# A one-core hybrid layer in split fp32: GpSimd's block sums spread over two stages, the branch product's first operands issued by GpSimd, its gates loaded three groups ahead

## The chip, the cores and the metric

The kernel runs on one core of a Trainium2 chip. The metric is the device time of one execution in microseconds (us). Five engines run side by side, each in its own order: TensorE (PE), VectorE (DVE), ScalarE (ACT), GpSimd (POOL) and SyncE (SP), which here does nothing but issue DMA transfers. GpSimd issues transfers too, among them all that add to what is in memory (accumulating DMA). The transfers themselves run on 16 DMA engines that all issuers share.

## The reference

One layer of a streaming encoder, for a prompt of 1024 frames and a sample of 32, with model width 1024, all in float32:

```
h = RMSNorm(x)
z = h @ W_in -> [q_A k_A v_A | q_B f_B i_B og_B | gate_A gate_B]
A: windowed grouped-query attention on q_A k_A v_A            -> y_A
B: HGRN2 gated linear recurrence, 8 heads of width 128        -> y_B
m = sigmoid(gate_A) * (y_A @ W_brA) + sigmoid(gate_B) * (y_B @ W_brB)
x = x + RMSNorm(m @ W_out)
[a|u] = RMSNorm(x) @ W_up;  a = causal conv3(a)
x = x + RMSNorm((gelu(a) * u) @ W_down)                       (d_ff = 2816)
x = x + (p @ W_ple) * sigmoid(x @ W_ple_gate)
```

Besides x it returns the last window rows of k and v, the recurrence's final states and the convolution's tail.

## The kernel before

Each fp32 product is made of three matmuls on split operands (high by high, high by low, low by high). The large products also use a block scheme of seven products for a 2 by 2 block matrix in place of eight, so that some operands are sums of blocks of a weight or of an activation. Most weight sums are made on VectorE and GpSimd from tiles that were loaded. For W_down, for the branch weight W_brA and for y_A, they are made by GpSimd's DMA instead: a transfer with an adding write puts them into tensors in memory, `w_d` (W_down, 704 KB a transfer), `wa_d` (W_brA, 1024 KB) and `sa_d` (y_A, whose tensor is `ya_d`, 1056 KB). `dv`, `av` and `ya_v` are views of W_down, W_brA and y_A by blocks.

The stages in time, by the profile:
- to about 350 us: norm, attention and the first gates (tiles `ya`, `hs`, `gt`; the stores `tb_d<-gt`, `ta_d<-gt`). Per pair of heads `ya` is stored to `ya_d`, and its negated halves to `sa_d`;
- 353 to 857 us: stage B. Eight heads, each a unit of products for q and f, one for i and og, and the recurrence in blocks. The program is a list `pieces` of product steps; `at(m, f)` hangs a small job on piece m. Each unit's weights come by `b_raw` (L1027, tile `wu`, 512 KB each, on SP), are summed and split, and VectorE makes from the products the tiles `tf`, `vt`, `qx` and the state `S`. GpSimd zeroes tiles (`tq`, `d`, `kk`), copies part of `ke`, loads `S` and issues the sums;
- 857 to 869 us: the last three gate units, `stream(tail[3:], small)`, where `small` hangs jobs on half units: loads (`a_load`) and splits (`a_split`) of the first operands `oa` of the branch product, and weights (`a_prepare`);
- from 876 us: the branch product (`a_unit`; matmuls at L1597 to L1601 into `st`), whose gates come back from memory by `a_gate` as `ta`;
- 1060 to 1200: W_out and the mix; 1200 to 1616: the up stage, 22 units of about 20 us (`up_unit`); then down, and from 1850 the per-layer input.

The order on each engine is set by the order in which the program is written and by a scheduler; `behind(E, V, G)` keeps an instruction behind the last ones written for those engines, as an order and without a semaphore. GpSimd so runs ahead until an instruction of its own has to wait. Of the 45 sums in stage B, 32 are of W_down (four parts `c` of eight sums `n`), at piece 8 + 5(4n + c); 13 are of y_A and W_brA, at piece 10 + 12n. The lines that set this:

```
for n, (o, a, h, other) in enumerate(w_sums):
    for c in range(4):
        ...
        at(8 + 5 * (4 * n + c), w_sum)
...
    at(10 + 12 * n, a_sum)
```

Of the kernel before, what the change touches and what calls it, by code (L numbers as in the profile page):

```python
# [10 lines left out]
F32 = mybir.dt.float32  # L11
# [6 lines left out]
P = 128  # L18
# [12 lines left out]
H = 264  # L31
# [28 lines left out]
def layer_kernel(  # L60
# [229 lines left out]
    def gtile():  # L290
        return lp.tile([P, GMAX], F32, tag="gt", name=nm("gt"), bufs=2)
# [25 lines left out]
    with right("ap") as ap:  # L317
# [226 lines left out]
        def values(i, js):  # L544

            kv, ya = i // 4, yas[i]
            o = o8.pop(i) if js[0] == 8 else o_bank()
            m_ = span(js[0])[0]
            for x, j in enumerate(js):
                ph, pl = probs.pop((i, j))  # L550
                tl = span(j)[4]
                oc = o[:, x * 256:x * 256 + 2 * m_]
                for a, (vt_, _, _) in enumerate(tl):
                    lhs = Vs[:, vt_, kv].rearrange("p a b -> p (a b)")
                    z = slice(2 * a * m_, 2 * (a + 1) * m_)
                    E.matmul(oc, lhs, ph[:, z], start=a == 0, stop=False)
                    E.matmul(oc, lhs, pl[:, z], start=False, stop=a == len(tl) - 1)
            nx = len(js)
            u = aq.tile([P, 2, 2, P], F32, tag="u", name=nm("u"), bufs=1)
            o4 = o[:, :nx * 2 * m_].rearrange("p (x h q) -> p x h q", x=nx, h=2)  # L560
            t0 = 1024 if js[0] == 8 else js[0] * P
            y3 = ya[:, t0:t0 + nx * m_].rearrange("p (x q) -> p x q", x=nx)
            S.copy(u[:, :nx, :, :m_], o4)
            V.tensor_tensor(y3[0:64], o4[0:64, :, 0, :], u[64:128, :nx, 0, :m_], op=ALU.add)
            V.tensor_tensor(y3[64:128], o4[64:128, :, 1, :], u[0:64, :nx, 1, :m_], op=ALU.add)
            if js[-1] == 8:
                dma(ya_d[:, i], ya[:])
                for p in range(2):
                    nt, o = gtile(), H * (2 * p + 1 - i // 4)
                    S.mul(nt[:, :H], ya[:, o:o + H], -1.0)  # L570
                    for q in ((4, 3) if i < 4 else (5,)):
                        dma(sa_d[q][:, i % 4, p], nt[:, :H])

        def h_sums(k):


            hs = [aq.tile([P, 384], F32, tag=f"hs{a}", name=nm("hs")) for a in range(4)]
# [508 lines left out]
    with right("bp") as bp:  # L1086
# [351 lines left out]
        def more():  # L1438
# [4 lines left out]
        at(len(pieces) - 2, more)  # L1443
        w_sums = [(3, 0, 0, None), (4, 0, 1, None), (1, 0, 0, None), (6, 1, 0, None),
                  (3, 0, 1, None), (4, 1, 1, None), (1, None, None, 4), (6, None, None, 1)]
        for n, (o, a, h, other) in enumerate(w_sums):
            for c in range(4):
                def w_sum(o=o, src=w_d[other][:, c] if other else dv[:, a, h, c], c=c,
                          op={"accum_op": ALU.add} if n > 3 else {}):
                    with behind(E, V, G):  # L1450
                        gdma(w_d[o][:, c], src, **op)
                at(8 + 5 * (4 * n + c), w_sum)
        a_sums = [(3, av[:, 0, 0], 0), (4, av[:, 0, 1], 0), (1, av[:, 0, 0], 0), (6, av[:, 1, 0], 0),
                  (3, av[:, 0, 1], 1), (4, av[:, 1, 1], 1), (1, wa_d[4][:], 1), (6, wa_d[1][:], 1)]
        y_sums = [(4, ya_v[:, 0, 0], 1), (3, ya_v[:, 1, 1], 1), (1, sa_d[4][:], 0),
                  (1, ya_v[:, 1, 1], 1), (5, sa_d[1][:], 1)]
        for n, (dst, (o, src, acc)) in enumerate([(sa_d, y) for y in y_sums] + [(wa_d, a) for a in a_sums]):
            def a_sum(dst=dst[o], src=src, op={"accum_op": ALU.add} if acc else {}):
                with behind(E, V, G):
                    gdma(dst[:], src, max_dma_last_dim=4224, **op)  # L1460
# [62 lines left out]

    opa = {}

    def a_load(i, p):
        t = opa[i, p] = page_at(at_a[i][p], [P, 2, 4, H], "oa")
        src = sa_d[i][:, :, p] if i in sa_d else ya_v[:, min(i, 1), i // 6][:, :, p]
        dma(t[:, 1].bitcast(F32), src)

    def halves(hi, lo):
        S.copy(hi, lo.bitcast(F32))
# [18 lines left out]
    pctx.close()  # L1551
# [3 lines left out]
    with right("mp") as mp:  # L1555
# [11 lines left out]
        Ra, Rb, Ya, Yb = [None] * 4, [None] * 4, [None] * 4, [None] * 4  # L1567
        R_ = page_at("l6", [P, 4, 2, H], "R").bitcast(F32)

        def a_gate(col, h, sl):  # L1570
            t = mp.tile([P, 2, H], F32, tag="ta", name=nm("ta"), bufs=4)
            dma(t[:, sl], ta_d[col].rearrange("p (t h c) -> p h t c", t=2, h=2)[:, h, sl])
            return t

        def a_unit(ph, c, tps=(0, 1), ws=None, beside=None):
# [9 lines left out]
            for n, i in enumerate(OPS[ph]):  # L1585
                if ws is None:
                    a_prepare(n_a[0] + 5)
                    w = ready_a[n_a[0]]
                    n_a[0] += 1
                else:  # L1590
                    w = ws[n]
                kept.append(w)
                t, first = banks[i]
                for p in tps:
                    o, x = t[:, p, 0:H], opa[i, p]
                    for k in range(4):
                        E.matmul(o, w[:, 0, k], x[:, 0, k], start=first and k == 0, stop=False,  # L1597
                                 skip_group_check=True)
                        E.matmul(o, w[:, 0, k], x[:, 1, k], start=False, stop=False,
                                 skip_group_check=True)  # L1600
                        E.matmul(o, w[:, 1, k], x[:, 0, k], start=False, stop=k == 3,  # L1601
                                 skip_group_check=True)
                x, r = t[:, sl, 0:H], R_[:, c, sl]
                if i == 0:
                    d["s"], d["ta"] = tmp("as"), a_gate(c, 0, sl)
                    S.copy(d["s"][:, sl], x)
                elif i == 1:
                    V.tensor_tensor(r, x, d["s"][:, sl], op=ALU.subtract)
                elif i == 2:
                    ta = d["ta"]  # L1610
                    V.scalar_tensor_tensor(ta[:, sl], ta[:, sl], 1.0, x, op0=ALU.add, op1=ALU.mult)
                    gdma(mx_d[:, 0, c, sl], ta[:, sl])
                elif i == 3:
                    d["c"] = tmp("ac")
                    V.tensor_tensor(d["c"][:], r, x, op=ALU.subtract)
                elif i == 4:
                    e, ta = d["c"], a_gate(c + 4, 1, sl)
                    V.tensor_tensor(e[:], e[:], x, op=ALU.subtract)
                    V.scalar_tensor_tensor(ta[:], ta[:], 1.0, e[:], op0=ALU.add, op1=ALU.mult)
                    gdma(mx_d[:, 1, c], ta[:])  # L1620
                else:
                    e, ta = tmp("ac"), a_gate(*((c + 4, 0) if i == 5 else (c, 1)), sl)
                    V.tensor_tensor(e[:], *((r, x) if i == 5 else (x, r)), op=ALU.subtract)
                    V.scalar_tensor_tensor(M_[i][:, c], ta[:], 1.0, e[:], op0=ALU.add, op1=ALU.mult)
                if beside:
                    beside(n)
            return kept

        steps_a = {}

        def during(s, f, *a):
# [19 lines left out]
        for n, (i, p) in enumerate(((1, 1), (2, 1), (3, 0), (3, 1))):  # L1651
            during(n + n // 2, both, a_split, i, p)
# [606 lines left out]
    def up_unit(u):  # L2259
# [62 lines left out]
        for ps, steps in (((0,), first_), ((1,), early)) if u == 0 else (((0, 1), order),):  # L2322
            for n, (i, t, first, then) in enumerate(steps):
# [518 lines left out]
```

## Time and profile before

| | |
|---|---|
| median of 3 runs (lowest, highest) | 1982.41 us (1981.38, 1985.9) |
| the profiled execution | 1977.89 us, span 1976.2 us |
| its mean granted TensorE clock | 0.994 |
| busy: PE, DVE, ACT, POOL | 1935.5, 1452.8, 1011.4, 300.8 us |
| moved by DMA | 302.19 MB, mean 153 GB/s |

The profile is of one execution. Its rows name an engine, a line (L1027), an operation and the tiles out<-in. In a timeline, a bracket at the end of a row is the idle time of that engine ahead of the instruction and what ended it. A row of waits gives the waiting engine and line, what it waited for, and the total, count and longest in us. In the chain that ended last a row gives a start, a length and the work. A row by stretches gives the limits, the length, the busy time of the engines, then the granted clock (1.00 is full), the mean busy share of the DMA engines and GB/s. "SPq" is a queue that issues DMA; a row with x2 stands for two issues and their joint time.

### The profile page before, as it was taken

The numbers are of one execution on the slowest core, as the hardware profiler recorded it, in microseconds if no ns is written. First come the engines' busy times: TensorE is split into PE (matmuls) and PEld (weight loads), VectorE is DVE, ScalarE is ACT, GpSimd is POOL, SyncE is SP. The second block draws the span as 40 slices with busy tenths as digits, with TensorE's granted clock in tenths as the row PEclk, the third lists the DMA queues.
The fourth block names the chain that finished last, engine by engine and source line by source line (L and its number), as shares of the span: only waits on it lengthen the run. The fifth ranks groups of instructions, "written<-read, shape, count | busy, mean of one in ns | idle before, by whom it ended". The sixth has DMA issues, their size and how long they took to land.

```text
span 1976.2 us, 38048 instructions
## 1 busy us (share of the span) xinstructions
PE 1935.5 (98%) x14619; PEld 1916.4 (97%) x14619; DVE 1452.8 (74%) x3160; ACT 1011.4 (51%) x2182; POOL 300.8 (15%) x414
## 2 busy tenths in 40 slices
PE   8999999899999999989999999999999999999998
PEld 8999999899999999989999999999999999999998
DVE  6777777688888788747755678877878786668872
ACT  7667777466666656644223664333333345534432
POOL 2111211011112100000001023233343320000000
PEclk9999999999999999989999999999999999999999
DMA  8544544745749942268757583332333347655443
GB/s 267 150 114 115 138 128 104 213 114 170 160 109 159 176 108 73 90 219 271 212 158 264 166 306 103 108 110 87 119 99 110 109 142 253 206 186 160 118 133 88
DMA packets 311403, 302.19 MB, mean 153 GB/s; under 512 B 14293, under 2 KB 278904, under 8 KB 311221
## 3 DMA queue, kind: packets, MB, share of 16 engines
q1 hardware_dynamic: 279909, 232.27, 37.9%
q0 software_dynamic: 31184, 67.43, 14.5%
q8 instruction: 115, 1.88, 0.4%
q14 instruction: 67, 0.55, 0.1%
q10 hardware_dynamic: 128, 0.06, 0.0%
HBM read 213.48 MB, written 115.16 MB: 166 GB/s over the span
## 4 chain that ended last, share of the span: by engine, by line
PE 77%; DVE 9%; DMA 6%; ACT 4%; issue 3%; POOL 0%; SPq 0%; ACTq 0%; DVEq 0%; POOLq 0%
PE st L2278 7%; PE st L2276 7%; PE st L2277 7%; PE mm L205 5%; PE mm L207 5%; PE mm L206 5%; PE st L2395 4%; PE st L2397 4%; PE st L2396 4%; DMA wu<-in_w_in_dram 2%; PE G L1121 2%; PE G L1120 2%; PE G L1118 2%; PE Y L1118 2%; PE Y L1121 2%
## 5 line engine op out<-in xcount | busy, mean ns | idle before, releaser
L2276 PE MATMUL st<-op,wt 128*128 128x264 f32 x1232 | 349.0, 283 | 2.5 <-ACT Sp L2287 1.4
L2278 PE MATMUL st<-op,wt 128*128 128x264 f32 x1232 | 349.9, 284 | 0.0
L2277 PE MATMUL st<-op,wt 128*128 128x264 f32 x1232 | 347.9, 282 | 0.0
L2276 PEld LDWEIGHTS st<-op,wt 128*128 128x128 f32 x1232 | 231.3, 188 | 4.0 <-ACT Sp L2287 2.0
L2277 PEld LDWEIGHTS st<-op,wt 128*128 128x128 f32 x1232 | 231.4, 188 | 0.0
L2278 PEld LDWEIGHTS st<-op,wt 128*128 128x128 f32 x1232 | 230.9, 187 | 0.0
L2395 PE MATMUL st<-dop,wt 128*128 128x264 f32 x616 | 174.5, 284 | 1.2 <-ACT S L2410 1.2
L2397 PE MATMUL st<-dop,wt 128*128 128x264 f32 x616 | 174.4, 283 | 0.0
L2396 PE MATMUL st<-dop,wt 128*128 128x264 f32 x616 | 174.0, 283 | 0.0
L1944 ACT CAST wt<-wu 128x512 fp32r<-128x512 f32 x126 | 75.9, 618 | 178.1 <-POOL ab L2262 75.5
L205 PE MATMUL mm<-La,wh 128*128 128x384 f32 (+1 forms) x480 | 158.5, 331 | 0.4 <-DVE pl L229 0.4
L206 PE MATMUL mm<-Lb,wh 128*128 128x384 f32 (+1 forms) x480 | 155.3, 324 | 0.6 <-DVE Lb L780 0.6
L207 PE MATMUL mm<-La,wl 128*128 128x384 f32 (+1 forms) x480 | 155.0, 323 | 0.1
L1945 DVE TENSOR_TENSOR wt<-wu,wt 128x512 fp32r<-128x512 f32 x126 | 86.4, 694 | 46.7 <-ACT wt L1944 46.7
L2395 PEld LDWEIGHTS st<-dop,wt 128*128 128x128 f32 x616 | 115.6, 188 | 1.6 <-ACT S L2410 1.4
L2396 PEld LDWEIGHTS st<-dop,wt 128*128 128x128 f32 x616 | 115.7, 188 | 0.0
L2397 PEld LDWEIGHTS st<-dop,wt 128*128 128x128 f32 x616 | 115.5, 188 | 0.0
L2050 ACT CAST wt<-wd 128x512 fp32r<-128x512 f32 (+1 forms) x84 | 49.1, 586 | 91.2 <-PE st L2397 69.5
L1039 ACT CAST wt<-wu 128x512 fp32r<-128x512 f32 x108 | 64.8, 617 | 58.1 <-DVE wu L1047 25.3
L1040 DVE TENSOR_TENSOR wt<-wu,wt 128x512 fp32r<-128x512 f32 x108 | 72.5, 685 | 27.2 <-ACT wt L1039 26.9
L206 PEld LDWEIGHTS mm<-Lb,wh 128*128 128x128 f32 x480 | 90.5, 189 | 1.7 <-DVE Lb L780 1.4
L205 PEld LDWEIGHTS mm<-La,wh 128*128 128x128 f32 x480 | 90.3, 188 | 0.7 <-DVE pl L229 0.6
(600 smaller groups left out, 6294.0 us busy)
## 6 DMA issues: line engine op xcount, KB each, us to landing
wu<-in_w_up_dram SPq DMA_DIRECT2D x42, 512.0 KB
wu<-in_w_in_dram SPq DMA_DIRECT2D x36, 512.0 KB
w_d<-in_w_down_dram POOLq DMA_DIRECT2D x24, 704.0 KB, 11.0
a_d<-Up SPq DMA_DIRECT2D x22, 528.0 KB
wr<-in_w_in_dram SPq DMA_DIRECT2D x21, 512.0 KB
s_d<-sm SPq DMA_DIRECT2D x40, 264.0 KB
dop<-s_d SPq DMA_DIRECT2D x16, 528.0 KB
wr<-in_w_out_dram SPq DMA_DIRECT2D x16, 512.0 KB
```

The costliest lines, as they stand in the source:

```text
L205: E.matmul(ps, wh, a, start=first and n == 0, stop=False)
L206: E.matmul(ps, wh, b, start=False, stop=False)
L207: E.matmul(ps, wl, a, start=False, stop=last and n == len(ks) - 1)
L1118: E.matmul(o, wh, x[0][k], start=first and k == 0, stop=False, skip_group_check=True)
L1121: E.matmul(o, wl, x[0][k], start=False, stop=k == 3, skip_group_check=True)
L1945: V.tensor_tensor(t[:, 1], src, t[:, 0].bitcast(F32), op=ALU.subtract)
L2276: E.matmul(o, wh, xh, start=first and k == 0, stop=False, skip_group_check=True)
L2277: E.matmul(o, wh, xl, start=False, stop=False, skip_group_check=True)
L2278: E.matmul(o, wl, xh, start=False, stop=k == 3, skip_group_check=True)
L2395: E.matmul(o, wh, xh_, start=first and k == 0, stop=False, skip_group_check=True)
L2396: E.matmul(o, wh, xl_, start=False, stop=False, skip_group_check=True)
L2397: E.matmul(o, wl, xh_, start=False, stop=k == ng - 1, skip_group_check=True)
```

## The change

Four things are changed.

1. The sums in stage B. 16 of the 32 W_down sums (parts 0 and 1) stay in stage B, interleaved with the other 13 in one list, a sum every 5.5 pieces from piece 26 to 180. The other 16 (parts 2 and 3) go to the up stage, one in each of the units 2 to 17. All have `max_dma_last_dim=4224` now, so that a `w_d<-w_d` sum is cut into rows of 704 elements and not of 1408.
2. The first five operands of the branch product are issued by GpSimd, ahead of the last gate units. The other three stay on SP and are issued beside those units. The splits (`a_split`) come one half unit earlier, five of them instead of four in this stretch.
3. `a_gate` holds a queue: the gates of three groups are loaded ahead, and it is filled again after each group.
4. The negated halves of `ya` use the buffers of `hs` instead of those of `gt`.

```diff
-                    nt, o = gtile(), H * (2 * p + 1 - i // 4)
+                    nt = aq.tile([P, GMAX], F32, tag=f"hs{p}", name=nm("nt"), bufs=1)
+                    o = H * (2 * p + 1 - i // 4)
...
-        for n, (o, a, h, other) in enumerate(w_sums):
-            for c in range(4):
-                def w_sum(o=o, src=..., c=c, op={"accum_op": ALU.add} if n > 3 else {}):
-                    with behind(E, V, G):
-                        gdma(w_d[o][:, c], src, **op)
-                at(8 + 5 * (4 * n + c), w_sum)
+        def block_sum(dst, src, acc):
+            with behind(E, V, G):
+                gdma(dst, src, max_dma_last_dim=4224, **({"accum_op": ALU.add} if acc else {}))
+        def w_sum(n, c):
+            o, a, h, other = w_sums[n]
+            block_sum(w_d[o][:, c], w_d[other][:, c] if other else dv[:, a, h, c], n > 3)
...
+        sums = [lambda n=n, c=c: w_sum(n, c) for n in range(8) for c in range(2)]
         for n, (dst, (o, src, acc)) in enumerate(... y_sums ... a_sums ...):
-            def a_sum(...): ...
-            at(10 + 12 * n, a_sum)
+            sums.insert(2 * n, lambda d=dst[o][:], src=src, acc=acc: block_sum(d, src, acc))
+        for n, f in enumerate(sums):
+            at(26 + 11 * n // 2, f)
...
-    small = {0: [lambda i=i, p=p: a_load(i, p) for p in range(2) for i in range(3)]}
-    small[0] += [lambda p=p: a_load(3, p) for p in range(2)]
-    for m in range(4):
-        p, i = divmod(m, 3)
-        small.setdefault(m + 2, []).append(lambda i=i, p=p: both(a_split, i, p))
-    for m in range(3):
-        small.setdefault(m + 1, []).insert(0, lambda m=m: both(a_prepare, m))
+    first_a = [(i, p) for p in range(2) for i in range(3)]
+    for i, p in first_a[:5]:
+        a_load(i, p, gdma)
+    for m, (i, p) in enumerate(first_a[:5]):
+        small[m + 1] = [lambda i=i, p=p: both(a_split, i, p)]
+    for m in range(3):
+        small[m + 1].append(lambda m=m: both(a_prepare, m))
+    for m, (i, p) in enumerate(((2, 1), (3, 0), (3, 1))):
+        small[m + 3].append(lambda i=i, p=p: a_load(i, p))
...
-        def a_gate(col, h, sl):
+        def a_gate(col, h, tps):
+            while len(ta_a) < 3 and gates_a:
+                c_, h_, p_ = gates_a.pop(0)
+                t = mp.tile([P, 2, H], F32, tag="ta", name=nm("ta"), bufs=4)
+                ...
+                ta_a.append(((c_, h_, p_), t))
...
+                if 2 <= u < 18 and n == 4:
+                    w_sum((u - 2) // 2, 2 + u % 2)
```

What it does to the order is shown at three places. A row is a line, an operation and the tiles with their running numbers, in the order in which the engine takes them.

GpSimd at the first head of stage B (`tq`, `d` are zeroed tiles, `ke` is the copy that PE transposes later). Before:

```order
L1451 DMA w_d_131<-in_w_down_dram 128x11x128
L1460 DMA sa_d_110<-ya_d 1024x1x264
L1451 DMA w_d_131<-in_w_down_dram 128x11x128
L1254 MEMSET tq_5070 128x96
L1451 DMA w_d_131<-in_w_down_dram 128x11x128
L1460 DMA sa_d_109<-ya_d 1024x1x264
L1451 DMA w_d_131<-in_w_down_dram 128x11x128
L1451 DMA w_d_132<-in_w_down_dram 128x11x128
L1254 MEMSET d_949_5369 128x96
L1303 COPY ke_5370<-vt_5286 128x32
```

After:

```order
L1255 MEMSET tq_5070 128x96
L1449 DMA sa_d_110<-ya_d 1024x1x264
L1255 MEMSET d_949_5366 128x96
L1304 COPY ke_5367<-vt_5283 128x32
L1255 MEMSET tq_5560 128x96
L1449 DMA w_d_131<-in_w_down_dram 128x11x128
```

Seven sums stood ahead of the copy, one does now.

GpSimd at head 4, from one copy of `ke` to the next. Before:

```order
L1303 COPY ke_8273<-vt_8189 128x32
L1254 MEMSET tq_8463 128x96
L1311 MEMSET kk_8575 32x128
L1312 MEMSET kk_8575 64x128
L1460 DMA wa_d_106<-in_w_br_a_dram 512x1x512
L1451 DMA w_d_130<-w_d_132 128x1408
L1460 DMA wa_d_104<-wa_d_106 256x1024
L1451 DMA w_d_130<-w_d_132 128x1408
L1451 DMA w_d_133<-w_d_130 128x1408
L1324 DMA S_8795<-in_state_hgrn_dram 128x128
L1451 DMA w_d_130<-w_d_132 128x1408
L1254 MEMSET d_1550_8941 128x96
```

After:

```order
L1304 COPY ke_8259<-vt_8174 128x32
L1255 MEMSET tq_8447 128x96
L1449 DMA w_d_132<-in_w_down_dram 128x11x128
L1312 MEMSET kk_8559 32x128
L1313 MEMSET kk_8559 64x128
L1449 DMA w_d_131<-in_w_down_dram 128x11x128
L1325 DMA S_8778<-in_state_hgrn_dram 128x128
L1449 DMA wa_d_106<-in_w_br_a_dram 512x1x512
L1255 MEMSET d_1550_8924 128x96
L1449 DMA wa_d_104<-wa_d_106 256x1024
L1304 COPY ke_8925<-vt_8805 128x32
L1449 DMA w_d_130<-w_d_132 128x2x704
```

Six sums became four, and the load of the state S comes ahead of two of them.

ACT at the start of the branch product (`oa` casts are the splits of its operands, `wt` those of its weights, `gt` the last three gates, the third of which frees the bank that the first branch matmul writes). Before:

```order
L297 ACTIVATE gt_10904<-X_10863 128x288
L1532 CAST oa_10876<-oa_10876 128x1056
L297 ACTIVATE gt_10946<-Y_10916 128x384
L1532 CAST oa_10878<-oa_10878 128x1056
L1532 CAST oa_10880<-oa_10880 128x1056
L297 ACTIVATE gt_10984<-Z_10957 128x384
L1532 CAST oa_10882<-oa_10882 128x1056
```

After (weights' casts in between, as before, not shown):

```order
L297 ACTIVATE gt_10882<-X_10857 128x288
L1534 CAST oa_10847<-oa_10847 128x1056
L297 ACTIVATE gt_10926<-Y_10896 128x384
L1534 CAST oa_10849<-oa_10849 128x1056
L1534 CAST oa_10851<-oa_10851 128x1056
L1534 CAST oa_10853<-oa_10853 128x1056
L297 ACTIVATE gt_10968<-Z_10939 128x384
L1534 CAST oa_10855<-oa_10855 128x1056
```

The last gate now stands behind four casts of operands, all four loaded by GpSimd, where it stood behind three. On SP the store `tb_d<-gt` of the first of these gates now stands behind one load of `oa` instead of eight.

More of the change, by code (lines that the diff above doesn't have):

```diff
@@ L574, in h_sums @@
         def h_sums(k):
-            hs = [aq.tile([P, 384], F32, tag=f"hs{a}", name=nm("hs")) for a in range(4)]
+            hs = [aq.tile([P, GMAX], F32, tag=f"hs{a}", name=nm("hs"), bufs=1) for a in range(4)]
             b11, b12, b21, b22 = (t[:] for t in hs)
@@ L1568, in layer_kernel @@
         R_ = page_at("l6", [P, 4, 2, H], "R").bitcast(F32)
-        def a_gate(col, h, sl):
-            t = mp.tile([P, 2, H], F32, tag="ta", name=nm("ta"), bufs=4)
-            dma(t[:, sl], ta_d[col].rearrange("p (t h c) -> p h t c", t=2, h=2)[:, h, sl])
+        tps_a = [(0, (0,)), (1, (0,)), (0, (1,)), (1, (1,)), (2, (0, 1)), (3, (0, 1))]
+        gates_a = [(c, 0, tps) for c, tps in tps_a]
+        gates_a += [(a, h, (0, 1)) for c in range(4) for a, h in ((c + 4, 1), (c + 4, 0), (c, 1))]
+        ta_a = []
+        def a_gate(col, h, tps):
+            while len(ta_a) < 3 and gates_a:
+                c_, h_, p_ = gates_a.pop(0)
+                t = mp.tile([P, 2, H], F32, tag="ta", name=nm("ta"), bufs=4)
+                z_ = slice(p_[0], p_[-1] + 1)
+                dma(t[:, z_], ta_d[c_].rearrange("p (t h c) -> p h t c", t=2, h=2)[:, h_, z_])
+                ta_a.append(((c_, h_, p_), t))
+            if col is None:
+                return
+            key, t = ta_a.pop(0)
+            assert key == (col, h, tuple(tps))
             return t
@@ L1604, in a_unit @@
                 if i == 0:
[L1605 removed]
+                    d["s"] = tmp("as")
                     S.copy(d["s"][:, sl], x)
@@ L1627, in a_unit @@
             return kept
+        a_gate(None, 0, ())
         steps_a = {}
@@ L1650, in layer_kernel @@
             during(9 + n + n // 2, both, a_split, i, p)
-        for n, (i, p) in enumerate(((1, 1), (2, 1), (3, 0), (3, 1))):
-            during(n + n // 2, both, a_split, i, p)
+        for n, (i, p) in enumerate(((2, 1), (3, 0), (3, 1))):
+            during(2 * n + 1, both, a_split, i, p)
         for n in range(4):
```

17 lines of the change are left out of this document (7 added, 10 removed).

## The prediction

> **What bounds the kernel now.** I read the page first (span, engines, granted clock), then the waits of TensorE (PE), then the chain that ended last, and then the timeline around each wait that is both long and near something the change touches.
>
> ```profile
> span 1976.2 us, 38048 instructions
> PE 1935.5 (98%) x14619; PEld 1916.4 (97%) x14619; DVE 1452.8 (74%) x3160; ACT 1011.4 (51%) x2182; POOL 300.8 (15%) x414
> ```
>
> PE is busy for 1935.5 of 1976.2 us. The change removes no matmul, so all it can win is idle time, 40.7 us in the whole kernel, and the half-speed stretches that idle time brings. The waits of PE, with the line and operation that each was waiting for:
>
> ```profile
> PE st L1597 <- ACT gt L297: 7.8, 1, 7.8
> PE so L1367 <- DVE S L1347: 5.5, 2, 4.8
> PE Z L1118 <- DVE tf L1146: 5.1, 1, 5.1
> ...
> PE Y L1118 <- DVE vt L1139: 2.2, 1, 2.2
> ```
>
> They are single places (a 5.5 that is one of 4.8 and a small one). The chain that ended last puts a late DMA at the three longest:
>
> ```profile
> 359.86 20.29 DMA wu<-in_w_in_dram
> ...
> 682.28 10.97 DMA out_dram<-S
> ...
> 867.43 8.49 DMA tb_d<-gt
> ```
>
> So this is a kernel at its matmuls' pace with three holes, at 376, 689 and 869 us, all made by late transfers. I price each hole and then what the moved work could cost where it goes.
>
> **The change, hole one: the first head of stage B (first GpSimd sums).** The rows below are SP's, POOL's (GpSimd's), ACT's and PE's own, then two stretches with PE busy time, granted clock, DMA share and GB/s, and the size of a wu load.
>
> ```profile
> 359.33 19.05 SPq L1027 DMA_DIRECT2D wu<-in_w_in_dram  x4
> 355.96 1.45 POOL L1460 DMA_DIRECT2D sa_d<-ya_d  x1 [17.83 <-DMA ya_d<-ya]
> 356.97 2.59 POOL L1451 DMA_DIRECT2D w_d<-in_w_down_dram  x2
> 378.63 0.62 ACT L1039 CAST wt<-wu 128x512 fp32r<-128x512 f32 x1 [10.49 <-DMA wu<-in_w_in_dram]
> 381.48 0.66 PE L1118 MATMUL Z<-La,wt 128*128 128x384 f32 x1 [5.12 <-DVE tf L1146]
> 397.68 0.44 PE L1118 MATMUL Y<-TH,wt 128*128 128x384 f32 x1 [2.15 <-DVE vt L1139]
> 383.09:386.51 3.42, 3.42 (x13) 0.50 0.01 2
> 386.51:389.92 3.41, 3.41 (x24) 1.00 0.00 0
> wu<-in_w_in_dram SPq DMA_DIRECT2D x36, 512.0 KB
> ```
>
> GpSimd issues one ya sum and two w_down sums at 356 to 359.6 us, just as SP issues four loads of wu; the cast needs wu and has it at 378.6, 19 us later. In the new order GpSimd issues a single sum ahead of the copy of ke of this head, and that one already stands before the 355.96 wait; the one in the row above and both w_down sums come only after the copy. The wait therefore loses its cause: four loads of 512 KB (2.1 MB), at the 358 GB/s that a crowded stretch reaches further below, take 5.9 us from 359.3, and were wanted by about 373.5 (381.48 less 5.12 less the 2.85 from cast to matmul). Saved: 5.1 us of wait. The clock fell to 0.50 after that idle time and the matmuls from 381.48 to 386.51 ran at half speed: 5.0 us that would take 2.5, so 2.5 more. The vt wait at 397.7 is VectorE still catching up with the late wu; I give back 1.0 of its 2.15 (bounds 0 and 2.15). Term one: 5.1 + 2.5 + 1.0 = 8.6.
>
> The Trainium skill, "TensorE: Matmul & The Clock Gate", Part 1, says that the clock is halved after an idle window of 3.4 us, returns after a busy one, and that these windows run freely. The rows above agree: the grid of 3.41 us fits the changes of the clock, and the share at half speed ends on it. It gives the same 2.5 us.
>
> **Hole two: head 4.**
>
> ```profile
> 666.81 4.58 SPq L1027 DMA_DIRECT2D wu<-in_w_in_dram  x2
> 671.12 2.00 POOL L1451 DMA_DIRECT2D w_d<-w_d  x2
> 682.28 0.36 SPq L1352 DMA_DIRECT2D out_dram<-S  x1
> 693.36 0.35 DVE L1347 SCALAR_TENSOR_TENSOR S<-S,dec,so 128x128 f32<-128x128 f32 x1 [6.72 <-DMA out_dram<-S]
> 693.76 0.80 PE L1367 MATMUL so<-z,z 128*128 128x128 f32 x2 [4.85 <-DVE S L1347]
> 672.00:692.00 20.00, 16.91 (x113) 16.56 (x111) 13.34 (x43) 14.91 (x38) 2.76 (x5) 1.00 1.06 228
> 693.71:697.12 3.41, 3.36 (x13) 0.50 0.34 92
> 659.78 0.49 PE L1367 MATMUL so<-vk,am 128*128 128x128 f32 x2 [0.61 <-DVE S L1347]
> ```
>
> The state's small store out_dram<-S is issued at 682.28 and lands 11 us later, because it stands behind two wu loads and five sums that crowd the engines (DMA share 1.06 over 20 us at only 228 GB/s). VectorE may not overwrite S before that, and PE waits 4.85. In the new order four sums stand between the copies of ke of this head and the next instead of six, with the load of S ahead of two of them, and the w_d<-w_d sums come behind the second copy, in rows of 704 elements (2,816 B) instead of 1408. Over stage B the sums fall from 45 in 163 pieces to 29 in 155. I take the wait as gone: 4.85, plus 0.6 at 659.78 (same cause), plus 3.4 us at half clock, worth 1.7. Term two: 7.1; bounds 0 (it merely moves to the next cluster) and 7.2.
>
> **Hole three: the start of the branch product.**
>
> ```profile
> 864.00:876.00 12.00, 4.80 (x28) 4.48 (x26) 4.89 (x5) 4.24 (x6) 0.00 (x0) 0.80 1.10 358
> 867.16 1.08 ACT L1532 CAST oa<-oa 128x1056 fp32r<-128x1056 f32 x1
> 876.02 0.49 ACT L297 ACTIVATE gt<-Z 128x384 f32<-128x384 f32 x1 [7.79 <-DMA tb_d<-gt]
> 868.47 0.34 PE L207 MATMUL Z<-La,wl 128*128 128x384 f32 x1
> 876.57 0.59 PE L1597 MATMUL st<-oa,wt 128*128 128x264 f32 x1 [7.76 <-ACT gt L297]
> 878.02:881.44 3.42, 3.42 (x18) 0.50 0.85 229
> 890.91 0.43 DVE L1611 SCALAR_TENSOR_TENSOR ta<-ta,st 128x264 f32<-128x264 f32 x1 [4.07 <-DMA ta<-ta_d]
> 894.20 0.36 PE L1597 MATMUL st<-oa,wt 128*128 128x264 f32 x1 [0.65 <-DVE R L1608]
> oa<-ya_d SPq DMA_DIRECT2D x6, 528.0 KB
> ```
>
> The first branch matmul waits for the last gate (gt from Z), whose buffer is held by tb_d<-gt, a store that SP issues behind eight loads of 528 KB (0.54 MB). The engines are full at 358 GB/s, so the loads themselves take 8 x 1.51 = 12.1 us. The change gives five to GpSimd and puts the store on SP behind one load only. But ACT's new order has the casts of four GpSimd loads ahead of that gate, one more than before. If the two queues share the engines evenly, the fourth GpSimd load lands after 4 x 3.02 = 12.1 us from 860.6, at 872.7; cast 1.08 and gate 0.5 make PE start at about 874.3 instead of 876.6. Saved: 2.2, and 0.5 of the slow clock (4.87 us at half speed become some 3.7). Gates three groups ahead remove the 4.07 that VectorE waited for ta and the 0.65 that PE waited after it: 0.65. Term three: 3.4. Bounds: 0.6 (loads land no sooner) and 10.2 (GpSimd's four get the full rate and land at 866.7, so PE only waits for Z and its gate, 869.4: 7.2 + 2.4 + 0.6). I take the even split, since no row here shows one queue preferred.
>
> Against this part speaks the Trainium skill, "DMA: Bandwidth & Descriptors", Rules for kernel authors: it says that spreading transfers over several issuing engines does not help bandwidth, since all use the same 16 DMA engines, and saves only issue time. The 358 GB/s at a DMA share of 1.10 agrees with it here. By it alone the sum would lose 2.7 of term three; what it leaves out is which transfer comes first.
>
> **What the moved work costs elsewhere.** Sixteen w_down sums go to the up stage, one each in 16 units.
>
> ```profile
> 407.00 1.05 POOL L1451 DMA_DIRECT2D w_d<-in_w_down_dram  x1
> 1301.98 1.29 POOL L1958 TENSOR_TENSOR wu<-wu 128x512 f32<-128x512 f32 x1 [3.94 <-DVE wt L1945]
> 1300.00:1350.00 50.00, 50.00 (x416) 50.00 (x415) 40.74 (x65) 16.32 (x25) 16.03 (x11) 1.00 0.32 110
> w_d<-in_w_down_dram POOLq DMA_DIRECT2D x24, 704.0 KB, 11.0
> 406.57 0.37 POOL L1303 COPY ke<-vt 128x32 f32<-128x32 f32 x1 [46.83 <-DVE d L1257]
> ```
>
> An issue holds GpSimd for 1.05 us, and behind it in the unit stand only a memset and L1958, which idles 3.94 us first; 0.72 MB in 20 us is 36 GB/s more on a stage at 110, whose DMA share is 0.32. Cost 0, cover 2.9 us; if the cover is gone the up matmuls wait by what exceeds it. Bounds: -1 and +21 (below). Copies of ke that now stand behind sums: the copy above waited 46.83 us for its data and GpSimd had nothing else to do, so cost 0; a late one would show as a wait of PE at L1305. The negated ya halves leave the ring of gt tiles for two of the hs buffers: 0, bounds -1 and +1, since the list of waits shows none of PE in attention above a microsecond. Down: same bytes, 0.
>
> The sum is 8.6 + 7.1 + 3.4 = 19.1 us. The profiled execution took 1977.9 us (span 1976.2 and 1.7 around it), which is 0.23% under the median of the runs, 1982.4. It would become 1958.8. Taken from the median: 1963.3 us.
>
> **Rivals.** (A) GpSimd's loads get the engines almost alone and hole three closes but for the gate: 10.2 instead of 3.4, sum 25.9, 1956.5 us. For it: SP's competing loads also wait for room in its own queue, as the 4.58 us for two wu issues shows. Against: three oa loads of SP's are still there.
> (B) The fourth GpSimd load lands only with the last of the eight, its cast and the gate come when they do now, and term three is 0.65: sum 16.4, 1966.0 us. For it: the 358 GB/s, which no order of issue raises; against: the store that the gate waits for no longer queues behind eight loads. It is what the rule on spreading would give.
> (C) Head 4 still collides: the new order has wa_d sums and w_d<-w_d sums next to each other there, and the second waits for the first to land. If they crowd the wu loads as at 672 to 692, 5 us of term two stay: sum 14.1, 1968.3 us. Against: two of the six sums are gone from that stretch, and the long rows with them.
> (D) The change does not do what it says: the wu loads are late because of their own 2.1 MB and head 4 because of S's load, and the sum is about 0 to 3: 1980 to 1982. Against: 2.1 MB in 19 us is 0.11 TB/s, far below 358 GB/s.
> (E) The other side: in the up stage the issue hits GpSimd where the next unit's weights wait for it. Each of the 16 units would have to lose over 1.2 us to eat 19.1; this begins only when issue and descriptor work exceed 3.94 us a unit. At 5.3 us (3.94 plus 1.35) it would cost 16 x 1.35 = 21.6, so 1984.9 us. Against: 1.05 us in the row, and no wait of PE for GpSimd in the list.
>
> **How the numbers follow.** Main case 0.44, A 0.20, B 0.13, C 0.14, D 0.05, E 0.04. The likeliest gives 1963. Two in ten may lie outside: D and E with 0.09, and the outer parts of A and C; the bounds of single terms, and 0.2% for the level of the runs (1981.4 to 1985.9, which is also about what a measurement of this kernel can tell from no change), widen 1956.5 to 1953 and 1968.3 to 1972. Faster by over 0.2% is main, A, B, C and the near part of D, 0.92; within 0.2% the rest of D, 0.04; slower is E, 0.04.
>
> **What would show it.** After the change PE should have no wait at its matmul of Z for tf near 376 and the loads of wu there should be under 10 us; out_dram<-S near 682 should land within 4 us and no half-clock stretch follow; the first branch matmul should wait for gt some 5 us (main), under 1 (A) or 7 to 8 (B); no wait for ta; the up stage should keep its 20 us a unit with PE at 50.00 of 50 us. The prediction is wrong if a new wait of PE for ke, for wu in the up stage or for the ya halves in attention appears with more than 2 us, or if the hole of head 4 is back at another head.

## The result, and the profile after

The changed kernel takes 1954.43 us (median of 4 runs, 1954.02 to 1955.39) against 1982.12 (median of 4, 1981.38 to 1985.9): a ratio of 0.9857, 95% interval 0.984 to 0.9874, 27.7 us less. It is inside the range and below the forecast of 1963 by 8.6. Its profiled execution took 1954.29 us (span 1952.5).

The page of the changed kernel (span and busy time) and the list of its PE waits:

```profile
span 1952.5 us, 38068 instructions
PE 1929.3 (99%) x14619; PEld 1911.8 (98%) x14619; DVE 1452.2 (74%) x3160; ACT 1012.4 (52%) x2182; POOL 308.5 (16%) x419
```

```profile
PE st L1616 <- ACT gt L297: 5.0, 1, 5.0
PE tr L744 <- POOL ident masks.py:199: 2.6, 1, 2.6
PE st L2297 <- ACT Sp L2308: 1.4, 2, 1.0
PE st L2418 <- ACT S L2433: 1.2, 1, 1.2
PE tr L2816 <- ACT xs L2811: 1.1, 1, 1.1
PE Y L1119 <- DVE vt L1140: 1.0, 1, 1.0
```

Of the long waits of before, tf (5.1) and S (4.8) are gone from the list, vt fell from 2.2 to 1.0, and the gate at the branch's start from 7.8 to 5.0. PE is also 6.2 us less busy (1935.5 to 1929.3) with the same number of matmuls. Most of that is time at half clock: by the clock's records 13.3 us of PE's busy time ran at half speed before and 3.1 us now, and half of the difference is 5.1 us.

Both programs issue the same 14,619 matmuls, in one order but for a dozen that stand a few places off. So the start of the same matmul can be taken from two traces, and the difference tells where the time went. The table gives the length of stretches between such matmuls, for all kernels of this study (the columns' limits in the time of before; up: 1200 to 1626; the branch column runs on to 1173, so that what is won at its start and lost later cancels). It is worked out from the traces' start times, so that each place is compared with itself:

```
us                 0-72  72-218  339-375  375-407  652-714   859-901  859-1173      up
                  start  attent.  B start hole one hole two  branch   branch+
before            69.85  145.53    36.30    32.01    62.73    41.63    313.94   425.58
before, again     68.21  145.53    36.31    35.39    63.12    42.17    314.48   425.57
changed           68.89  144.60    35.16    23.20    55.14    37.68    309.99   425.60
sums_only         68.21  145.53    35.15    22.76    55.13    40.48    312.79   425.60
loads_only        68.95  145.94    36.63    33.88    64.09    39.37    311.68   425.55
neg_gates_only    70.18  144.62    35.51    33.45    63.38    40.85    313.16   425.55
rows_only         69.36  145.51    36.16    32.12    62.98    42.00    314.31   425.57
spread_old_rows   68.22  144.59    35.15    22.78    55.13    37.83    310.19   425.58
late_start        69.70  145.36    35.56    22.78    64.77    40.99    313.30   425.58
up_double         68.50  144.58    35.16    22.78    55.14    38.72    311.02   425.53
gate_first        69.81  144.60    35.16    22.78    55.13    37.71    310.02   425.56
weights_first     67.80  144.61    35.15    22.78    55.13    40.66    317.77   426.24
five_on_sp        69.43  144.58    35.16    22.78    55.13    35.70    309.52   425.55
weights_ahead     69.54  144.73    35.16    22.79    55.13    37.50    310.37   425.54
```

From before to changed: start 1.0 (it differs by 2.4 among the kernels without any change there, so this is scatter), attention 0.9, start of stage B 1.1, hole one 8.8, hole two 7.6, branch 4.0, the rest within 0.1: together 23.4 of the 23.7 by which the span fell. The branch's 4.0 has the most scatter after the start: to 901 us the kernels in which neither its loads nor its gates were changed differ by 1.7 (40.48 to 42.17).

The places in the changed kernel. Hole one: a stretch (PE, PEld, DVE, ACT, POOL busy, clock, DMA share, GB/s) before and after, GpSimd's timeline after, and ACT's casts of wu after.

```profile
362.00:378.00 16.00, 14.35 (x92) 14.12 (x90) 7.85 (x12) 5.05 (x9) 0.00 (x0) 1.00 1.09 254
```

```profile
362.00:378.00 16.00, 16.00 (x104) 16.00 (x103) 12.72 (x21) 9.56 (x16) 0.00 (x0) 1.00 0.28 80
```

```profile
394.75 0.37 POOL L1304 COPY ke<-vt 128x32 f32<-128x32 f32 x1 [60.60 <-DVE d L1258]
...
395.60 1.14 POOL L1449 DMA_DIRECT2D w_d<-in_w_down_dram  x1 [0.32 <-issue]
```

```profile
364.50 1.14 ACT L1040 CAST wt<-wu 128x512 fp32r<-128x512 f32 x2
```

The stretch that moved 254 GB/s at a DMA share of 1.09 now moves 80 at 0.28, PE is busy for all of it, the next sum comes only behind the copy of ke, at 395.6, and ACT has the second pair of wu at 364.5 without a wait, 8.5 us after SP began to issue (355.98).

Hole two: SP's store of S, the next write of S by VectorE, and the stretch around the store's issue.

```profile
669.60 0.36 SPq L1353 DMA_DIRECT2D out_dram<-S  x1
```

```profile
673.87 0.33 DVE L1348 SCALAR_TENSOR_TENSOR S<-S,dec,so 128x128 f32<-128x128 f32 x1
```

```profile
648.00:672.00 24.00, 24.00 (x165) 23.93 (x163) 18.19 (x51) 17.71 (x46) 4.07 (x5) 1.00 0.44 81
```

The store lands within the 4.3 us up to the write (the row has no bracket: nothing was waited for); it took 11 us before. The 20 us that began at 672 before begin, from the same matmul on, at 659 now: PE is busy for all of them, and the engines move 97 GB/s at a share of 0.50, after 228 at 1.06.

Hole three: ACT, PE, two stretches of 3.41 us (PE busy, clock, DMA share, GB/s), and the landing times of GpSimd's five loads.

```profile
852.85 1.07 ACT L1534 CAST oa<-oa 128x1056 fp32r<-128x1056 f32 x1 [0.63 <-DMA oa<-ya_d]
853.83 0.48 ACT L297 ACTIVATE gt<-Z 128x384 f32<-128x384 f32 x1
```

```profile
854.37 0.59 PE L1616 MATMUL st<-oa,wt 128*128 128x264 f32 x1 [4.97 <-ACT gt L297]
```

```profile
851.00:854.41 3.41, 0.04 (x1) 0.94 1.05 357
854.41:857.82 3.41, 3.41 (x17) 0.56 0.96 275
```

```profile
DMA to landing us min/median/max: 4.7/7.5/10.6
```

As priced, the last gate stands directly behind the cast of the fourth GpSimd load, which waits for its DMA, and PE behind the gate. At half speed PE is now busy for 3.1 us (in the clock's window from 854.0 to 857.4) instead of 4.9.

### The profile page after: what moved, and what is told of

The parts are those of the page before. It is cut to its first block, busy times and chain, and to the rows that moved or that the text cites. A ratio compares the mean times of both kernels' runs of the same rounds, so it can differ in the third digit from the quotient of the medians.

```text
span 1952.5 us, 38068 instructions
## 1 busy us (share of the span) xinstructions
PE 1929.3 (99%) x14619; PEld 1911.8 (98%) x14619; DVE 1452.2 (74%) x3160; ACT 1012.4 (52%) x2182; POOL 308.5 (16%) x419
## 4 chain that ended last, share of the span: by engine, by line
PE 86%; DVE 5%; DMA 3%; ACT 3%; issue 2%; POOL 0%; SPq 0%; ACTq 0%; DVEq 0%; POOLq 0%
PE st L2299 7%; PE st L2298 7%; PE st L2297 7%; PE mm L205 6%; PE mm L206 6%; PE mm L207 6%; PE st L2418 4%; PE st L2420 4%; PE st L2419 4%; PE Y L1119 2%; PE G L1122 2%; PE st L205 2%; PE G L1121 2%; PE Y L1122 2%; PE Y L1121 2%; PE G L1119 2%
## 5 line engine op out<-in xcount | busy, mean ns | idle before, releaser
L1965 ACT CAST wt<-wu 128x512 fp32r<-128x512 f32 x126 | 75.9, 618 | 178.1 <-POOL wu L1974 71.6
L1966 DVE TENSOR_TENSOR wt<-wu,wt 128x512 fp32r<-128x512 f32 x126 | 86.5, 695 | 46.7 <-ACT wt L1965 46.7
L207 PEld LDWEIGHTS mm<-La,wl 128*128 128x128 f32 x480 | 90.2, 188 | 0.5 <-DVE wl L756 0.5
L1119 PE MATMUL G<-La,wt 128*128 128x288 f32 x288 | 90.4, 314 | 0.0
```

The source lines that it names most:

```text
L207: E.matmul(ps, wl, a, start=False, stop=last and n == len(ks) - 1)
L1119: E.matmul(o, wh, x[0][k], start=first and k == 0, stop=False, skip_group_check=True)
L1966: V.tensor_tensor(t[:, 1], src, t[:, 0].bitcast(F32), op=ALU.subtract)
```

## The experiments

**Is the level of before a matter of one hole?**

> The kernel before once more, unchanged, for a second profile. Its profiled execution took 1977.9 us, 3.5 to 8 us less than the runs that were timed, while the changed kernel's agrees with its own runs to 0.2 us. Theory 1, the holes vary: this profile has the same three holes (376, 689, 869 us) and one of them, or a new one of the same kind (a wait for wu or for a store behind a crowd of transfers), is some 4 us longer. Theory 2, the level varies: every stage is longer by the same 0.2%, with no hole that differs by over 1 us.

Its profiled execution took 1980.03 us (span 1978.3). Its waits:

```profile
PE st L1597 <- ACT gt L297: 8.0, 1, 8.0
PE Z L1118 <- DVE tf L1146: 7.0, 1, 7.0
PE so L1367 <- DVE S L1347: 5.5, 2, 5.0
```

This is theory 1. Hole one alone is 3.4 us longer than in the first profile (35.39 against 32.01), the others 0.4 and 0.5; every other stretch agrees but the start. The wait for tf is 1.9 us longer, and behind it a second stretch at half clock, of 3.4 us from 399.5, costs 1.7. In the five profiles that still have hole one as it was, that stretch takes 32.0 to 35.4 us; without it, 22.76 to 23.20. The kernel before ran between 1975 and 1987 us in the comparisons below. That all of this is hole one is not shown, since only profiled runs can be read by place.

**One part alone.** Three kernels, each the kernel before with a part of the change: the sums (both stages); the eight first loads; the negated halves in the hs buffers, with the gates ahead.

```diff
# sums_only: as in the change, list `sums`, block_sum, w_sum in up_unit
# loads_only
+    for i, p in first_a[:5]:
+        a_load(i, p, gdma)
...
# neg_gates_only
+                    nt = aq.tile([P, GMAX], F32, tag=f"hs{p}", name=nm("nt"), bufs=1)
...
+            while len(ta_a) < 3 and gates_a:
```

> Of the change only the sums are taken over: 29 in stage B, 16 in the up stage, rows of 704 elements. Theory 1, each hole has its own cause: holes one and two (wu at 376, out_dram<-S at 689) are gone, worth 9.9 and 7.6 us in the traces so far, the branch product still waits 7.8 us for the gate: 17.5 us less than before. Theory 2, hole one is closed by the earlier hs buffers and not by the sums: hole one stays, 7 to 8 us less.

1959.2 us against 1980.99, ratio 0.989 (0.9873 to 0.9906): 21.8 us less, 17.5 expected. Holes one and two are gone (22.76, 55.13), the start of stage B is 1.1 shorter, and the gate's wait stays:

```profile
PE st L1598 <- ACT gt L297: 7.6, 1, 7.6
```

The runs scatter from 1957.0 to 1963.5. In the traces the kernel is 20.9 us shorter than the first profile of before: 9.2 and 7.6 at the two holes, 1.1 at the start of stage B, 1.2 in the branch, and 1.6 at the kernel's start, which is scatter. Theory 2 is out: the hs buffers aren't in this kernel.

> Of the change only the eight first operands of the branch product are taken over: five loads on GpSimd, three on SP, splits earlier. Theory 1: holes one and two stay as before, the wait at the branch's start is about 5 us instead of 7.8, 3 us less in all. Theory 2, the shorter wait came from the stage before, which left the DMA engines less to do: the wait stays at 7 to 8 us and the time within 1 us of before.

1978.55 against 1980.99, ratio 0.9987 (0.9977 to 0.9996). Holes one and two stand, and the gate's wait is 5.1 us, as theory 1 said.

```profile
PE Z L1118 <- DVE tf L1146: 7.0, 1, 7.0
PE so L1367 <- DVE S L1347: 5.5, 2, 4.9
PE st L1600 <- ACT gt L297: 5.1, 1, 5.1
```

> Two parts of the change that lie far apart, read by place: the negated halves of ya in the buffers of hs (attention, before 350 us), and the gates of the branch product three groups ahead (after 876 us). Theory 1: attention is faster by 1 to 2 us, as the two traces differ there, and the 0.65 us after the wait for ta is gone: 1.5 to 2.7 us less in all. Theory 2: the difference in attention was scatter, 0.7 us less, all of it in the branch product.

1979.17 against 1980.99, ratio 0.9987 (0.9978 to 0.9996). Attention is 0.9 shorter, here and in every kernel with the hs buffers (144.58 to 144.73 against 145.36 to 145.94). In the list of ACT's waits of before, between 100 and 330 us, stands what this removes:

```profile
ACT gt L570 <- DMA ta_d<-gt: 3.8, 2, 3.5
```

The negation wanted a gt tile whose store had not landed. This wait is gone; two smaller ones, of 1.1 us together for the store of an hs tile, have come in its place. The gates' part: VectorE's wait for ta is gone, and so is PE's behind it (0.6 to 0.9 us in before, before again and rows_only, but 0.3 in sums_only and none in late_start); the stretch as a whole shows nothing, as it varies by 1.7 us (40.48 to 42.17) among kernels without it.

**Rows or spreading?**

```diff
# rows_only (the kernel before)
-                        gdma(w_d[o][:, c], src, **op)
+                        gdma(w_d[o][:, c], src, max_dma_last_dim=4224, **op)
# spread_old_rows (the changed kernel): w_sum issues without max_dma_last_dim
# late_start (the kernel before)
-                at(8 + 5 * (4 * n + c), w_sum)
+                at(26 + 5 * (4 * n + c), w_sum)
-            at(10 + 12 * n, a_sum)
+            at(28 + 12 * n if n else 10, a_sum)
```

> The kernel before with one edit: the W_down sums have the limit of 4224 bytes too, so that the eight w_d<-w_d sums go in rows of 704 elements (2,816 B) and not of 1408. The others, at the first head too, keep their rows of 128 elements. Theory 1, the row's length starves the small rows of wu and of the state's store: hole two (4.9 to 5.3 us of wait and 1.7 of slow clock) is gone, hole one stays: 7 us less. Theory 2, the number of bytes in flight does it: hole two stays within 1 us, and the time is that of before.

1978.63 against 1981.1, ratio 0.9989 (0.9979 to 0.9999). Both holes stay (32.12, 62.98), and so does the wait for S:

```profile
PE so L1367 <- DVE S L1347: 5.9, 2, 5.5
```

So the rows are not the cause, as theory 2 has it; what the bytes in flight do was not tried by this. The 2.5 us by the medians has no place in the trace. It is as much as loads_only and neg_gates_only won, so that these two parts are shown by their places and not by their times.

> The changed kernel, but the W_down sums keep the rows of 1408 elements where they add w_d to w_d. Theory 1, the rows' length was what closed hole two: it comes back there or at a later head, 5 to 7 us more than the changed kernel (1959 to 1961 us). Theory 2, spreading alone does: within 1 us of the changed kernel (1954.4).

1954.16 (1953.08 to 1956.0), as the changed kernel, and place by place the same. Theory 2 holds again: the shorter rows of the change are worth nothing here.

> The kernel before with all sums but the first of y_A moved 18 pieces later (W_down from piece 26, the others from piece 40), at the old rate of 45 sums in stage B and with the old rows. Theory 1, hole one is a matter of when the sums begin, hole two of what stands together at one head: hole one is gone (10 to 12 us less by 407 us), hole two stays or moves to another head. Theory 2, the rate does it: the loads of the next head's wu are late instead, and a wait of the same 5 to 7 us for tf or wu appears at head 1 or 2.

1970.2 against 1981.1, ratio 0.9946 (0.9931 to 0.9961). Hole one is gone at the full old rate, so it was a matter of when the sums begin. Hole two stays at its place, even 2 us longer, but with another victim. PE's wait; ACT, SP and GpSimd at that place; the stretch:

```profile
PE G L1118 <- DVE sg L1204: 8.1, 1, 8.1
```

```profile
698.56 0.41 ACT L1203 ACTIVATE sg<-G 128x288 f32<-128x288 f32 x1 [9.21 <-DMA yb_d<-sg]
```

```profile
680.44 20.85 SPq L1393 DMA_DIRECT2D yb_d<-sg  x3
```

```profile
681.90 1.66 POOL L1451 DMA_DIRECT2D w_d<-w_d  x2
```

```profile
684.00:700.00 16.00, 7.91 (x50) 7.60 (x49) 7.46 (x27) 5.49 (x14) 0.00 (x0) 0.86 0.89 204
```

Here it is the stores yb_d<-sg, 147 to 197 KB each, that stand behind wu and four sums, and ACT that may not write sg before. In before it was the 64 KB store of S and VectorE. So hole two is a small store whose tile is wanted back, caught in a crowd at the head where sums meet two wu loads; which store is a matter of a few microseconds. Neither theory had that. By the medians this kernel is 10.9 us faster, but its trace is only 6.9 us shorter than the first of before, as it also loses 1.8 us at 1183 to 1188 (in the time of before), where PE runs at half clock for 3.4 us; why is open.

**How much does the up stage cover?**

```diff
# up_double (the changed kernel)
-        sums = [lambda n=n, c=c: w_sum(n, c) for n in range(8) for c in range(2)]
+        sums = []
...
                     w_sum((u - 2) // 2, 2 + u % 2)
+                    w_sum((u - 2) // 2, u % 2)
```

> The changed kernel with all 32 W_down sums in the up stage, two in each of the units 2 to 17, one behind the other; stage B keeps the 13 sums of y_A and W_brA, at the same pieces. Theory 1, the cover behind the issue (2.9 to 4.7 us of idle GpSimd against 1.05 us an issue) holds for two: the up stage stays at 425.6 us and, as stage B has no hole left, the time stays within 1 us of the changed kernel. Theory 2, the second issue or the added 36 GB/s delays L1979 and with it the next weights: each of 16 units loses 0.3 us or more, 5 us in all.

1955.05 (1954.18 to 1957.05), no difference that can be told. The up stage takes 425.53 us. GpSimd in one unit, and the stretch:

```profile
1254.30 2.10 POOL L1449 DMA_DIRECT2D w_d<-in_w_down_dram  x2
1256.40 0.12 POOL L2283 MEMSET ab<- 128x2 f32 x1
1260.19 1.60 POOL L1979 TENSOR_TENSOR wu<-wu 128x512 f32<-128x512 f32 x1 [3.67 <-DVE wt L1966]
```

```profile
1220.00:1270.00 50.00, 50.00 (x415) 50.00 (x414) 39.04 (x66) 17.46 (x25) 19.14 (x16) 1.00 0.62 182
```

Two issues take 2.1 us, and L1979 still idles 3.67 first. This is theory 1. Rival E had the price of an issue right (1.05 us), and its threshold is out of reach even with two.

**What holds the branch's start?** Four edits of the changed kernel, of ACT's order and of the first loads.

```diff
# gate_first: splits of operands 3, 4, 5 behind the last gate unit
-        small[m + 1] = [lambda i=i, p=p: both(a_split, i, p)]
+        small[(1, 2, 5, 6, 7)[m]] = [lambda i=i, p=p: both(a_split, i, p)]
# weights_first: gate_first, first_a[:3] on GpSimd, the other five on SP behind the weights
# weights_ahead: gate_first, and
-        small[m + 1].append(lambda m=m: both(a_prepare, m))
+    small[0] = [lambda m=m: both(a_prepare, m) for m in range(4)]
# five_on_sp
-        a_load(i, p, gdma)
+        a_load(i, p)
```

> The changed kernel with the splits of the third, fourth and fifth operand moved behind the last gate unit, so that ACT evaluates the last gate before those three casts; the loads stay. Theory 1, the wait of 5.0 us at the branch's start is the gate standing behind the cast of the fourth operand: PE goes on at once (0.6 us of wait) and loses no clock, 6 us less by itself, of which some 3 come back at the fifth product, whose weights were split only at 858: 2 to 4 us less than the changed kernel (1950.5 to 1952.5). Theory 2, the DMA engines set the pace here whatever the order: what is won at the start is lost at the third product and the fifth, within 1 us of 1954.4.

1954.44 (1953.85 to 1956.31). The wait for the gate falls to 3.0, and 1.9 of new waits follow; to 901 us the stretch is 37.71 against 37.68. PE's waits there:

```profile
PE st L1616 <- ACT gt L297: 3.0, 1, 3.0
PE st L1616 <- ACT as L1625: 1.9, 2, 1.0
```

By the time this is theory 2, though the reason could still have been ACT's order (three weight casts stood between the second operand and the gate).

> As gate_first, and only three operands are loaded by GpSimd; the other five are issued by SP, held behind the weights of the fifth and sixth product. Theory 1: neither the gate nor the weights are late, and the whole start of the branch product loses its wait and its slow clock, 5 to 6 us less than the changed kernel (1948.5 to 1949.5). Theory 2, the DMA engines set the pace: the operands of the seventh product come late instead, and the time is that of gate_first or more.

1961.8 (1960.44 to 1963.89), 7 us more than the changed kernel, as theory 2 allowed. PE starts almost at once (1.3) and then stands for 5.8 us, as the operands moved to SP come late:

```profile
PE st L1620 <- ACT as L1629: 6.5, 2, 5.8
PE st L1620 <- DVE ac L1638: 2.5, 1, 2.5
PE st L1620 <- ACT gt L297: 1.3, 1, 1.3
```

```profile
856.77 1.07 ACT L1534 CAST oa<-oa 128x1056 fp32r<-128x1056 f32 x1 [2.94 <-DMA oa<-ya_d]
```

> The changed kernel with the first five operands issued by SP instead of GpSimd, at the same place of the program. Theory 1, it is GpSimd's own queue that helps, since the store of the first gate does not stand behind the loads: the wait at the branch's start goes back to 7 to 8 us, 2 to 4 us more than the changed kernel. Theory 2, what helped is that fewer loads go ahead (five on SP, not eight): the wait is 4 to 6 us and the time within 1 us of 1954.4.

1956.9 (1955.69 to 1957.36). The wait is 3.4 us, so GpSimd's queue is not what shortened it: it is that five loads go ahead of the store and not eight. What ends last is the store again, and not the fourth cast:

```profile
PE st L1616 <- ACT gt L297: 3.4, 1, 3.4
```

```profile
852.40 0.49 ACT L297 ACTIVATE gt<-Z 128x384 f32<-128x384 f32 x1 [1.56 <-DMA tb_d<-gt]
```

The time is 2.5 us more than the changed kernel's, which neither theory had. In the trace the start of the branch is 2.0 us shorter to 901 us (35.70 against 37.68), of which 1.5 are lost again by 1173, and another 0.7 is lost at 1856. Where the slower runs lose the rest stays open (the profiled execution, 1955.69, was the quickest of them).

> The changed kernel with the splits of the first four branch weights moved ahead of the last gate units, so that their buffers come free and the weights of the fifth and sixth product are loaded some 10 us sooner, and with the splits of the third to fifth operand behind the last gate. The loads on GpSimd stay five. Theory 1, ACT's order set the start: in gate_first the gate still stood behind three weight casts that followed a late operand, and the fifth product's weights were late since their load waited for those casts; now PE waits 1 to 2.5 us for the gate, no wait follows, and it is 3 to 4.5 us less than the changed kernel (1950 to 1951.5). Theory 2, the bytes that have to arrive set the pace: what is won at the gate is lost within the next ten products, within 1 us of 1954.4.

1955.05 (1953.89 to 1956.58). The weights are early, no wait follows, and yet the gate comes at 854.5, 5.2 us late: now its buffer is held again (the gates have two), by the store of the first gate that SP issued at 842.2 and that lands 12 us later in the crowd.

```profile
842.23 0.46 SPq L298 DMA_DIRECT2D tb_d<-gt  x1
```

```profile
854.48 0.49 ACT L297 ACTIVATE gt<-Z 128x384 f32<-128x384 f32 x1 [2.05 <-DMA tb_d<-gt]
```

Changed, gate_first and weights_ahead come to 309.99, 310.02 and 310.37 us by 1173. Three orders of ACT put the wait in three places at one price, as theory 2 has it. That the bytes set the pace agrees with 310 to 319 GB/s from 840 to 860 us in all three, and with weights_first, which moves 249 there and takes longer. It does not settle it: five_on_sp moves 294 there and is the quickest to 901. That nothing but fewer bytes would help is argued, not shown, as no run here moved fewer.

## Why the prediction was right, and where it was off

- Hole one: term 8.6, measured 8.8 (and 1.1 just ahead of it, not priced). The wait of 5.1 and 2.5 of slow clock are gone, and vt's wait gave 1.15 where 1.0 was taken. The cause was as said, and late_start shows that the beginning of the sums is enough to remove it. One reading was off: SP did not issue the four loads of wu together, as the third and fourth were issued only at 366.25 and 369.44 us. What came late by the chain is the load issued at 359.86, 20.3 us after it.
- Hole two: term 7.1 with an upper bound of 7.2, measured 7.6: 0.9 and 5.0 at the two waits, where their rows gave 0.6 and 4.85, and 1.7 of slow clock. Of the reasons given, the rows of 704 elements do nothing. Spreading the sums does it, but no run takes apart that four stand there instead of six, that the load of S comes ahead of two, and that the w_d<-w_d sums come behind the second copy. In the changed kernel wa_d sums do stand at that place, as rival C had it, and no wait came of it.
- Hole three: term 3.4, measured 4.0, in a place that scatters by 1.7. Of it 2.8 are wait and 0.9 slow clock (2.2 and 0.5 were taken), the rest PE's wait behind ta. The wait is 5.0 where about 5.5 was worked out, and the gate stands behind the fourth cast as the order had it. The fourth load landed 11.7 us after the first was issued (841.1 to 852.83), where 12.1 was worked out, but this is luck, as two errors cancel. The even split isn't what happened: by the packets of that stretch GpSimd's queue moved 2.67 of 3.89 MB, over two thirds, beside SP's. And four loads weren't all that it moved: 2.67 MB is nearly all five (2.70), so that the fifth took what the larger share gave. Rival A named the larger share rightly and drew the wrong end from it. Its reading of the 4.58 us for two wu issues was wrong too: each issue took 0.37, and between them SP waited 3.8 us for a matmul of PE. Rival B had the rate right, which no order raised, but the wait fell by 2.8 us all the same, as the store no longer stands behind eight loads (loads_only: 5.1).
- Attention: 0 was taken, 0.9 measured; ACT's wait for ta_d<-gt was there to be read, 3.5 us, off PE's list.
- Up stage: 0, measured 0.0 (425.58 to 425.60), as priced.
- The sum: 19.1 against 23.4 in the traces. The terms were 4.3 short: 1.3 in the three holes, 1.1 ahead of hole one, 0.9 in attention, and 1.0 at the kernel's start, which is scatter and so luck. Of the signs that were named, all came: no wait for tf or for ta, wu in under 10 us, the store of S within 4.3 (4 was named) and no slow clock behind it, 5 us of wait for gt, PE busy for all of the up stage, and no new wait of over 2 us.
- The other half of the miss is the step to the median. The profiled execution of before lay 4.5 us under the median that the prediction used, and I carried the saving over unchanged ("Taken from the median: 1963.3"). But part of what varies from run to run is, by the second profile, hole one, which the change removes: the runs of the changed kernel keep within 1.4 us. It isn't all that varies, as sums_only, without holes one and two, still ran from 1957.0 to 1963.5. Counting from the profiled execution, the same sum gave 1958.8; with the 4.3 us that the terms were short, 1954.5. That the number of rival A lies close (1956.5) is chance: its wait under 1 us did not come.

## What to carry to other kernels

When a stage runs at its matmuls' pace, look for small stores whose tile is wanted back: here a store of 64 KB behind a crowd of large transfers took 11 us, and PE waited 4.85 us behind it. Move the crowd to a stage with idle DMA engines rather than cutting its rows, and begin it after the first loads of the stage that needs them. A saving that removes a varying wait is better counted down to the time without it than from the median of runs that contain it. And where transfers fill the engines, moving the wait's position in an engine's order may move the wait and not the time: three orders of ACT had one price here, and one order of the loads (weights_first) cost 7 us.

## What was not expected of the hardware

The stretch of hole one, 32 to 35 us long, differed by 3.4 us between two profiles of the kernel before, and without the crowd by 0.4 among nine kernels (22.76 to 23.20). In the up stage a GpSimd issue of a W_down sum took about 1.05 us whether alone or in a pair (2.10 for two). From the issue of GpSimd's five loads to the landing of the fourth, its queue moved over two thirds of the bytes (2.67 of 3.89 MB), beside SP's. The sums themselves landed in a median of 6.8 and 7.4 us when spread, after 11.0 and 11.3, with the same bytes:

```profile
w_d<-in_w_down_dram POOLq DMA_DIRECT2D x24, 704.0 KB, 6.8
...
w_d<-w_d POOLq DMA_DIRECT2D x8, 704.0 KB, 7.4
```
